# Winograd sums T3 and T2 and the first value weights prepared earlier in a hybrid attention block

## Chip, cores and metric

The kernel runs on one core of a Trainium2 chip. The metric is the device time of one execution in microseconds (us); the time of a version is the median of its runs.

## The reference, cut to what is computed

One decoder layer on 1024 tokens of width 1024. A normed input `h` is multiplied by one wide weight matrix; its columns feed a dilated attention (8 heads of 64), a gated linear recurrence (4 heads of 128) and two gates. The two branches are merged, then come a gated FFN, a gated embedding input and a last norm.

```python
h = rmsnorm(x, norm_mix[i])
proj = h @ w_in[i]
qa, ka, va, qb, fb, ib, gb, gate_a, gate_b = jnp.split(proj, IN_SPLITS, axis=-1)
ya = dilated_attention(qa, ka, va)
yb = hgrn2(qb, fb, ib, gb, lb_all[i], hg_norm[i])
merged = sigmoid(gate_a) * (ya @ w_a_up[i]) + sigmoid(gate_b) * (yb @ w_b_up[i])
x = x + merged @ w_out[i]
...
```

The part that matters here is `h @ w_in`. The kernel multiplies by the un-normed `x * norm_mix` and scales each token's result by its `rsqrt(mean(x*x) + EPS)`, called `rs`, afterwards.

## The kernel before

**Precision.** Every operand of a product is split in a high half (a cast on ScalarE, to fp32r) and a low half (source minus high half, on VectorE), and a product is three matmuls: high by high, high by low, low by high. The splits are the main work of ScalarE and VectorE, and the operand's matmuls wait for both.

**The start (lines 343 to 442).** Eight tiles `xr8[k]` of x (128 channels by 1024 tokens) are loaded and split with the gain; ScalarE squares them and VectorE adds the squares into `sqs`. Meanwhile TensorE computes three gate tiles, then a fourth (`w_next`, banks `pt1` and `pt0`). `rstd_rep` (line 207) makes `rs`: for each half of the tokens one matmul with ones (L209) into a bank of PSUM, two ScalarE reads of that bank (L210, an Abs_reciprocal_sqrt, whose table is loaded first, and L211), and three VectorE steps of a Newton iteration (L203 to L205). Both halves use the same bank, `pt0`, so the second L209 must wait until both reads of the first are done. VectorE then empties the gate banks with `rs` (L439).

**The projection units (lines 279 to 340, 750 to 794).** Twenty tiles of the projections are computed in ten units of two tiles by Winograd's scheme: seven products of four blocks each, in the order 1, 5, 7, 2, 3, 4, 6. A unit is 7 products x 4 blocks x 3 matmuls = 84 matmuls of 512 columns. The right operands are made once, before and during the first unit, and kept for all ten: products 1, 2 and 3 use the split tiles as they are; 5 uses T1, 7 uses T3, 4 uses T4 and 6 uses T2, sums of quarters of the gained `xr8`:

```python
T1 = f[i][:, c1] - f[i][:, c0]            # VectorE, L245, into f[i][:, c0]
T3 = f[i + 4][:, c1] - f[i][:, c1]        # GpSimd, L249, into f[i][:, c1]
T2 = f[i + 4][:, c1] - T1                 # GpSimd, L261, into f[i + 4][:, c1]
T4 = f[i + 4][:, c0] - T2                 # VectorE, L262, into f[i + 4][:, c0]
```

Each is then split by `block` (line 232: cast L235 on ScalarE, low half L236 on VectorE). `start_rights(j, i)` (line 373) scales the tiles that it needs by `norm_mix` in place (L376) and makes block i of product j. The calls for product 5 stand ahead of `rs`'s use, those for 7, then 4 and 6, at line 753, behind the first unit's left operands. The left operands are sums of weights (GpSimd, L292 to L295), split as L299 and L300. The sum s34 (L293, L295) lies in the buffer that `sqs` held.

**After the units (lines 840 to 874).** `v_gemm(0, ...)` computes the values of the first four heads: eight tiles of 128 tokens, 24 matmuls of 256 columns each, 192 in all (L484 to L486), from two weight strips that `weight` loads, splits on GpSimd (L171) and on VectorE (L172). Then the first four attention rows (scores L525 and L526 into the one score bank `sp`, row maximum L538 on VectorE, exponential L542 on ScalarE, scaling L544 on GpSimd, transposes L565 on TensorE) run beside the next gate product.

**What sets the order.** The program is written once in Python; a scheduler in the framework orders the instructions of each engine by readiness in its own estimate, and every engine then runs its own list strictly in order. `issue_after` adds an order edge without a wait. A buffer is named by its slot number in a ring (`ring([41])` is slot 41), and a writer waits for the last reader of what lay in the slot before. The weight strips of the values lie before in the general rings: high halves in slots 3 and 4, which the last unit's left operands for products 7 and 2 use, and low halves in slots 8 and 6. Slot 8 also holds the result `e0` of the last unit until its store to DRAM is done.

Of the kernel before, what the change touches and what calls it, by code (L numbers as in the profile page):

```python
# [12 lines left out]
F32 = mybir.dt.float32  # L13
F32R = mybir.dt.float32r
U8 = mybir.dt.uint8
AF = mybir.ActivationFunctionType
# [4 lines left out]
P = 128  # L21
S = 1024
D = 1024
KD = D // P
# [20 lines left out]
SCALE_A, SCALE_B = 0.9, (1.6, 1.3, 1.3, 1.3, 1.0)  # L45
# [4 lines left out]
V_MIX, V_FFN, V_PLE, V_FIN, V_LB0, V_LB1, V_HGN = 0, 8, 16, 24, 32, 36, 40  # L50
# [65 lines left out]
def drain(gen):  # L116
    for _ in gen:
        pass
# [11 lines left out]
def block_kernel(ctx: ExitStack, tc: tile.TileContext, a: dict, out: bass.AP):  # L130
    nc = tc.nc
    pe, dve, act, pool = nc.tensor, nc.vector, nc.scalar, nc.gpsimd
# [7 lines left out]
    def ring(ids):  # L140
        return Ring(sb, [f"s{i}" for i in ids])
# [9 lines left out]
    ones = cp.tile([P, P], F32, name="ones")  # L151
    lmask = cp.tile([P, len(LEVELS), P // 2], U8, name="lmask")
    vec = cp.tile([P, NVEC], F32, name="vec")
# [12 lines left out]
    def weight(src, shape, hi_ring=None, lo_ring=None):  # L166
        raw = RAW.next(shape, F32, "wr")
        nc.sync.dma_start(raw, src)
        hi = (hi_ring or HI).next(shape, F32R, "wh")
        lo = (lo_ring or LO).next(shape, F32R, "wl")  # L170
        pool.tensor_scalar(hi, raw, 1.0, 0.0, ALU.mult, ALU.add)  # L171
        dve.tensor_sub(lo, raw, f32(hi))  # L172
        return hi, lo
# [33 lines left out]
    def rstd_rep(dst, sq, bank, inv, t1, t2, first=True):  # L207

        pe.matmul(bank, ones, sq, start=first, stop=True)  # L209
        act.activation(dst, bank, AF.Abs_reciprocal_sqrt, bias=eps, scale=inv)  # L210
        read = act.activation(t1, bank, AF.Identity, bias=eps, scale=inv)  # L211
        return read, newton(dst, t1, t2)
# [55 lines left out]
    RIGHT = {1: right_b11, 5: right_t1, 7: right_t3, 2: right_b21, 3: right_b22, 4: right_t4, 6: right_t2}  # L268
# [76 lines left out]
    MS = pring("pt0")  # L345
    TMP = ring([37, 38])
# [8 lines left out]
    xg, xr8 = [], []  # L355
    sqs = SQ.next([P, S], F32, "sqs")
    nc.scalar.dma_start(vec, a["vec"])
    scratch = cp.tile([P, 1], F32, name="scratch")
    act_engine = act.activation(scratch, eps, AF.Square).ins.engine

    warm = MS.next([P, 512], F32, "warm")
    for _ in range(WARM):
        pe.matmul(warm[:, :P], ones, ones, start=True, stop=True)
    w_start = [weight_parts(a["w_in"][20 + t], [P, KD, P]) for t in range(NTOGETHER)]
    both = ps.tile([P, 2, 512], F32, tag="sp", name="start")
    banks = [ps.tile([P, 512], F32, tag=t, name=f"start_{t}") for t in ("b0", "b1", "b2", "ov")]
# [5 lines left out]

    def start_rights(j, i):

        for k in {5: (i,), 7: (i + 4,)}.get(j, ()):
            act.activation(xr8[k], xr8[k], AF.Identity, scale=vec[:, V_MIX + k : V_MIX + k + 1])  # L376
        right[j][i] = RIGHT[j](xr8, i, 4, ring([TB[j][i]]))

    def latest(engine):

        return next(i for i in reversed(nc.cur_bb.bb.instructions) if i.engine == engine)
# [34 lines left out]
            nc.sync.dma_start(lm, a["lmask"])  # L416
            dve.tensor_copy(lmask, lm)

    rs = ring([46]).next([P, S], F32, "rs")
    t1, t2 = TMP.next([P, S], F32, "t"), TMP.next([P, S], F32, "t")  # L420
    for c in range(2):
        cs = slice(c * 512, c * 512 + 512)
        scale_read, _ = rstd_rep(rs[:, cs], sqs[:, cs], MS.next([P, 512], F32, "ms"), 1.0 / D, t1[:, cs], t2[:, cs])

    with tc.issue_after(last_sum.ins):
        w_next = weight(a["w_in"][20 + NTOGETHER], [P, KD, P], ring([45]), ring([48]))
        last_split = latest(last_sum.ins.engine)

    with tc.issue_after(last_split), tc.issue_after(last_square.ins):
        for i in range(4):  # L430
            start_rights(5, i)
    banks.append([ps.tile([P, 512], F32, tag=t, name=f"start_{t}") for t in ("pt1", "pt0")])
    for b, cs in zip(banks[-1], halves):
        gemm(b, w_next, xg, cs.start, 512, range(KD))
# [51 lines left out]
            pe.matmul(b, xl[:, ts_], hi[:, k % 4, :], start=False, stop=(k == KD - 1))  # L486
            yield 3 * 0.107

    def v_gemm(half, vs):
        wts = [weight(a["w_v"][half, j], [P, 4, 256]) for j in range(2)]  # L490
        for t in range(NTOK):
            if t % 2 == 0:
                vs.append(VR.next([P, 2, 4, 2, 64], F32R, "v"))
            v = vs[-1]
            b = MM.next([P, 512], F32, "mm")[:, :256]
            yield from nat_gemm(b, wts, t)
            bv = b.rearrange("p (h d) -> p h d", h=4)
            r = rn[:, t : t + 1]
            act.activation(v[:, t % 2, :, 0, :], bv, AF.Identity, scale=r)
            dve.scalar_tensor_tensor(  # L500
                v[:, t % 2, :, 1, :], bv, r, f32(v)[:, t % 2, :, 0, :], op0=ALU.mult, op1=ALU.subtract
            )
# [248 lines left out]
    with tc.issue_after(first_emptied.ins), tc.issue_after(scale_read.ins):  # L751
        proj_lead()
    with tc.issue_after(latest(last_sum.ins.engine)), tc.issue_after(scale_read.ins):
        for i in range(4):
            start_rights(7, i)
        for i in (3, 0, 1, 2):
            for j in (4, 6):
                start_rights(j, i)

    TG, EO = ring([37, 38, 39]), ring([40, 47, 8])  # L760

# [4 lines left out]

    rn = cp.tile([P, NTOK], F32, name="rn")
    for tiles in units:
        done = dict(proj_unit(right, TG))
        e0, e1 = (EO.next([P, S], F32, "pj") for _ in range(2))  # L770
        dve.tensor_add(e0[:, c1], done[3], done[6])
        dve.tensor_add(e1[:, c0], done[4], done[6])
        pool.tensor_add(e1[:, c1], done[7], done[6])
        if tiles[0] < 8:

            dve.scalar_tensor_tensor(e0[:, c0], done[2], -0.125, rs[:, c0], op0=ALU.mult, op1=ALU.mult)
            dve.scalar_tensor_tensor(e0[:, c1], e0[:, c1], -0.125, rs[:, c1], op0=ALU.mult, op1=ALU.mult)
        else:
            dve.tensor_mul(e0[:, c0], done[2], rs[:, c0])
            dve.tensor_mul(e0[:, c1], e0[:, c1], rs[:, c1])  # L780
        pool.tensor_mul(e1, e1, rs)
        if 8 <= tiles[0] < 16:
            hd = tiles[0] // 2 - 4
            k = EO.next([P, S], F32, "k")
            act.activation(e0, e0, AF.Sigmoid)
            pool.tensor_scalar(e0, e0, oml[:, hd : hd + 1], lb[:, hd : hd + 1], ALU.mult, ALU.add)
            pool.tensor_scalar(k, e0, -1.0, 1.0, ALU.mult, ALU.add)
            nc.sync.dma_start(hg_dram["k"][hd], k)
            for cs in halves:
                sg = EV.next([P, 512], F32, "sg")  # L790
                act.activation(sg, e1[:, cs], AF.Sigmoid)
                dve.tensor_mul(e1[:, cs], e1[:, cs], sg)
        for j, e in zip(tiles, (e0, e1)):
            nc.sync.dma_start(proj_dst(j), e)
        if tiles[0] == 6:

            diag = EO.next([P, NTOK, P], F32, "diag")
            rs3 = rs.rearrange("p (n t) -> p n t", n=NTOK)
            dve.tensor_mul(diag, rs3, ident.unsqueeze(1).to_broadcast([P, NTOK, P]))
            dve.tensor_reduce(out=rn, in_=diag, axis=mybir.AxisListType.X, op=ALU.add)  # L800
# [42 lines left out]
    MM = pring("b0", "b1", "b2")  # L843
    NB = ring([47]).next([P, S], F32, "nb")
    nc.sync.dma_start(NB, a["nb"])
    drain(v_gemm(0, vs[0]))
    RAW, HI, LO = ring([0, 1]), ring([3, 4]), ring([8, 6])
    rows = []
    add_gates(2)
    v_last = fill.add(v_gemm(1, vs[1]))  # L850
    fill.along(attend_rows(0, qk[0, 0], rows), SCALE_A)
    groups = [(p, h, g) for p in range(NPAIR) for h in range(2) for g in range(2)]
    for (p, h, g), after in zip(groups, groups[1:] + [None]):
        if (p, h, g) == (2, 0, 0):
# [537 lines left out]
```

## Time and profile before

| what | value |
|---|---|
| median of 3 runs (lowest, highest) | 1650.5 us (1648.26, 1650.99) |
| the profiled execution: time, span in the profile | 1653.13 us, 1651.3 us |
| TensorE (PE) busy | 1599.5 us, 97% of the span |
| VectorE (DVE), ScalarE (ACT), GpSimd (POOL) busy | 68%, 39%, 29% |
| mean granted clock of TensorE | 0.987 |

The profiled execution's own time is 1.8 us above its span. PE is the row to read: the others have room over the whole span, and what counts is where PE stands still and who ends that wait.

### The profile page before, as it was taken

The page shows a single profiled execution, that of the slowest core. Times are in us where ns is not written, and L with a number is a line of the kernel's source. Part 1 is how long each engine was busy: PE and PEld are TensorE (multiplying, and loading weights), DVE is VectorE, ACT ScalarE, POOL GpSimd, SP SyncE. Part 2 cuts the span into 40 slices and gives each one's busy share as a digit, 9 for nine tenths or more (in the row PEclk, how much of TensorE's full clock was granted, in tenths as well). Part 3 has the DMA queues.
Part 4 walks back from the last instruction along what each step waited for, and adds up shares of the span by engine and source line. Part 5 has one row for each costly group of instructions (what it writes and reads, how often), then busy time and mean ns, then how long its engine had stood idle before and what let it go on. Part 6 is the DMA issues. An engine that isn't in the chain of part 4 may idle for free.

```text
span 1651.3 us, 21727 instructions
## 1 busy us (share of the span) xinstructions
PE 1599.5 (97%) x7968; PEld 1334.9 (81%) x7968; DVE 1119.2 (68%) x1725; ACT 651.9 (39%) x1130; POOL 475.7 (29%) x357
## 2 busy tenths in 40 slices
PE   8899998999999999999998999999999999999996
PEld 7687776898897888888786878888888788878886
DVE  8855655568665567774648786667777757789536
ACT  6422333357653011532336333333333454454433
POOL 2555662223322111015353222223333201002214
PEclk9999998999999999999999999999999999999998
DMA  5233344223224232543434773224444677765102
GB/s 199 77 103 113 128 147 140 80 87 81 65 71 156 91 108 98 177 145 118 134 127 144 269 260 130 90 101 142 153 160 159 214 262 249 237 200 159 43 1 102
DMA packets 93419, 227.97 MB, mean 138 GB/s; under 512 B 10368, under 2 KB 19840, under 8 KB 93312
## 3 DMA queue, kind: packets, MB, share of 16 engines
q1 hardware_dynamic: 93168, 226.57, 41.3%
q8 instruction: 62, 1.02, 0.3%
q14 instruction: 45, 0.37, 0.1%
q10 hardware_dynamic: 144, 0.02, 0.0%
HBM read 164.16 MB, written 62.39 MB: 137 GB/s over the span
## 4 chain that ended last, share of the span: by engine, by line
PE 47%; DVE 6%; DMA 5%; issue 2%; POOL 1%; ACT 1%; SPq 0%; DVEq 0%; POOLq 0%
PE u L275 7%; PE u L276 7%; PE u L277 7%; PE mm L192 5%; PE mm L194 5%; PE mm L193 5%; PE dnb L275 2%; PE dnb L277 2%; PE dnb L276 2%; DVE B L236 1%; DMA s_dram<-ls 1%; PE g L666 1%; DMA ls<-w_dn 1%; DMA w<-s_dram 1%; DMA w<-w_dn 1%
## 5 line engine op out<-in xcount | busy, mean ns | idle before, releaser
L275 PE MATMUL u<-B,q 128*128 128x512 f32 x776 | 303.9, 394 | 8.3 <-ACT m L333 5.1
L276 PE MATMUL u<-B,q 128*128 128x512 f32 x776 | 304.3, 392 | 3.9 <-DVE B L236 3.9
L277 PE MATMUL u<-B,q 128*128 128x512 f32 x776 | 303.6, 391 | 2.9 <-DVE q L300 2.9
L275 PEld LDWEIGHTS u<-B,q 128*128 128x128 f32 x776 | 146.8, 189 | 44.1 <-ACT m L333 9.5
L276 PEld LDWEIGHTS u<-B,q 128*128 128x128 f32 x776 | 146.6, 189 | 35.3 <-DVE B L236 5.4
L277 PEld LDWEIGHTS u<-B,q 128*128 128x128 f32 x776 | 146.7, 189 | 34.1 <-DVE q L300 3.3
L192 PE MATMUL mm<-xh,wh 128*128 128x512 f32 (+1 forms) x352 | 138.6, 394 | 0.0
L299 ACT CAST q<-s 128x512 fp32r<-128x512 f32 x128 | 79.4, 622 | 148.9 <-PE u L277 132.9
L300 DVE TENSOR_TENSOR q<-s,q 128x512 fp32r<-128x512 f32 x128 | 107.3, 841 | 40.9 <-ACT q L299 40.1
L194 PE MATMUL mm<-xh,wl 128*128 128x512 f32 (+1 forms) x352 | 132.3, 376 | 0.1
L193 PE MATMUL mm<-xl,wh 128*128 128x512 f32 (+1 forms) x352 | 131.8, 374 | 0.0
L171 POOL TENSOR_SCALAR wh<-wr 128x1024 fp32r<-128x1024 f32 (+1 forms) x55 | 59.9, 1091 | 247.6 <-PE mm L193 104.7
L300 DVE TENSOR_TENSOR q<-w,q 128x512 fp32r<-128x512 f32 x96 | 91.9, 958 | 51.1 <-ACT q L299 51.0
L192 PE MATMUL mm<-h,wh 128*128 128x512 f32 (+1 forms) x296 | 114.7, 387 | 1.2 <-POOL wh L171 1.1
L193 PE MATMUL mm<-l,wh 128*128 128x512 f32 (+1 forms) x296 | 114.4, 386 | 0.9 <-DVE l L910 0.9
L194 PE MATMUL mm<-h,wl 128*128 128x512 f32 (+1 forms) x296 | 113.7, 385 | 0.0
L299 ACT CAST q<-w 128x512 fp32r<-128x512 f32 x96 | 59.7, 622 | 122.0 <-PE u L277 69.7
L544 POOL TENSOR_SCALAR p<-p,rd 128x128 f32<-128x128 f32 (+3 forms) x64 | 53.3, 835 | 143.3 <-DVE rd L543 123.8
L1103 POOL TENSOR_TENSOR us<-v 128x512 f32<-128x512 f32 x22 | 38.4, 1746 | 171.6 <-DVE v L337 158.7
L194 PEld LDWEIGHTS mm<-xh,wl 128*128 128x128 f32 x352 | 66.8, 190 | 12.0 <-DVE wl L172 0.5
L484 PE MATMUL mm<-wh,xh 128*128 128x256 f32 x256 | 76.4, 300 | 0.0
L294 POOL TENSOR_TENSOR s<-s,w 128x512 f32<-128x512 f32 x32 | 45.1, 1410 | 107.4 <-DVE s L292 88.2
(305 smaller groups left out, 3791.5 us busy)
## 6 DMA issues: line engine op xcount, KB each, us to landing
w<-w_gu SPq DMA_DIRECT2D x44, 512.0 KB, 3.9
t_dram<-t SPq DMA_DIRECT2D x44, 256.0 KB, 2.3
w<-w_in SPq DMA_DIRECT2D x20, 512.0 KB, 3.8
w<-w_dn SPq DMA_DIRECT2D x40, 256.0 KB, 3.3
st<-t_dram SPq DMA_DIRECT2D x20, 512.0 KB, 4.5
ls<-w_dn SPq DMA_DIRECT2D x32, 256.0 KB, 4.1
wr<-w_in SPq DMA_DIRECT2D x13, 512.0 KB, 3.7
sg_dram<-gt SPq DMA_DIRECT2D x24, 256.0 KB, 2.0
```

The source lines that it names most:

```text
L171: pool.tensor_scalar(hi, raw, 1.0, 0.0, ALU.mult, ALU.add)
L192: pe.matmul(dst, hi[:, k, :], xh[:, c0 : c0 + n], start=first and k == ks[0], stop=False)
L193: pe.matmul(dst, hi[:, k, :], xl[:, c0 : c0 + n], start=False, stop=False)
L194: pe.matmul(dst, lo[:, k, :], xh[:, c0 : c0 + n], start=False, stop=last and k == ks[-1])
L275: pe.matmul(dst, q[:, 0, k], bh, start=first and not more and k == 0, stop=False, skip_group_check=more)
L276: pe.matmul(dst, q[:, 0, k], bl, start=False, stop=False, skip_group_check=more)
L277: pe.matmul(dst, q[:, 1, k], bh, start=False, stop=end, skip_group_check=more)
L294: pool.tensor_sub(s2, s1, a11)
L299: act.copy(q[:, 0], left[m])
L300: dve.tensor_sub(q[:, 1], left[m], f32(q)[:, 0])
L484: pe.matmul(b, xh[:, ts_], hi[:, k % 4, :], start=(k == 0), stop=False)
L544: pool.tensor_scalar(pr[:, :n], pr[:, :n], rd, 0.0, ALU.mult, ALU.add)
```

## The change

It has two places.

At the start, all eight tiles are scaled in one go behind the last square, and the blocks for product 7 (T3) are made right behind those for product 5 (T1), ahead of the reads of the sums of squares. The sums T2, which T4 is made from, are made there too, on GpSimd, and handed on to `start_rights`. The blocks for 4 and 6 stay behind the first unit's left operands, in another order.

At the end of the units, the two weight strips of `v_gemm(0)` are loaded and split in the last unit, with slots of their own: 41 and 42 for the high halves, 43 and 44 for the low ones. These four held the T3 blocks, whose last reader is product 7 of the last unit. The first attention rows are ordered behind the last matmul of `v_gemm(0)`.

```diff
--- before.py
+++ after.py
@@ -360,7 +360,7 @@
 
     warm = MS.next([P, 512], F32, "warm")
     for _ in range(WARM):
-        pe.matmul(warm[:, :P], ones, ones, start=True, stop=True)
+        warm_up = pe.matmul(warm[:, :P], ones, ones, start=True, stop=True)
     w_start = [weight_parts(a["w_in"][20 + t], [P, KD, P]) for t in range(NTOGETHER)]
     both = ps.tile([P, 2, 512], F32, tag="sp", name="start")
     banks = [ps.tile([P, 512], F32, tag=t, name=f"start_{t}") for t in ("b0", "b1", "b2", "ov")]
@@ -372,9 +372,10 @@
 
     def start_rights(j, i):
 
-        for k in {5: (i,), 7: (i + 4,)}.get(j, ()):
-            act.activation(xr8[k], xr8[k], AF.Identity, scale=vec[:, V_MIX + k : V_MIX + k + 1])
-        right[j][i] = RIGHT[j](xr8, i, 4, ring([TB[j][i]]))
+        t2 = (xr8[i + 4][:, c1],) if j in (4, 6) else ()
+        right[j][i] = RIGHT[j](xr8, i, 4, ring([TB[j][i]]), *t2)
+
+    pe_engine = warm_up.ins.engine
 
     def latest(engine):
 
@@ -416,19 +417,31 @@
             nc.sync.dma_start(lm, a["lmask"])
             dve.tensor_copy(lmask, lm)
 
-    rs = ring([46]).next([P, S], F32, "rs")
-    t1, t2 = TMP.next([P, S], F32, "t"), TMP.next([P, S], F32, "t")
-    for c in range(2):
-        cs = slice(c * 512, c * 512 + 512)
-        scale_read, _ = rstd_rep(rs[:, cs], sqs[:, cs], MS.next([P, 512], F32, "ms"), 1.0 / D, t1[:, cs], t2[:, cs])
 
     with tc.issue_after(last_sum.ins):
         w_next = weight(a["w_in"][20 + NTOGETHER], [P, KD, P], ring([45]), ring([48]))
         last_split = latest(last_sum.ins.engine)
 
+
     with tc.issue_after(last_split), tc.issue_after(last_square.ins):
+        for k in range(KD):
+            act.activation(xr8[k], xr8[k], AF.Identity, scale=vec[:, V_MIX + k : V_MIX + k + 1])
+        scaled = latest(act_engine)
+    with tc.issue_after(scaled):
+        for j in (5, 7):
+            for i in range(4):
+                start_rights(j, i)
+            right_read, right_made = latest(act_engine), latest(last_sum.ins.engine)
         for i in range(4):
-            start_rights(5, i)
+            t2 = xr8[i + 4][:, c1]
+            pool.tensor_sub(t2, t2, xr8[i][:, c0])
+    rs = ring([46]).next([P, S], F32, "rs")
+    t1, t2 = TMP.next([P, S], F32, "t"), TMP.next([P, S], F32, "t")
+    with tc.issue_after(right_read), tc.issue_after(right_made):
+        for c in range(2):
+            cs = slice(c * 512, c * 512 + 512)
+            bank = MS.next([P, 512], F32, "ms")
+            scale_read, _ = rstd_rep(rs[:, cs], sqs[:, cs], bank, 1.0 / D, t1[:, cs], t2[:, cs])
     banks.append([ps.tile([P, 512], F32, tag=t, name=f"start_{t}") for t in ("pt1", "pt0")])
     for b, cs in zip(banks[-1], halves):
         gemm(b, w_next, xg, cs.start, 512, range(KD))
@@ -486,8 +499,8 @@
             pe.matmul(b, xl[:, ts_], hi[:, k % 4, :], start=False, stop=(k == KD - 1))
             yield 3 * 0.107
 
-    def v_gemm(half, vs):
-        wts = [weight(a["w_v"][half, j], [P, 4, 256]) for j in range(2)]
+    def v_gemm(half, vs, wts=None):
+        wts = wts or [weight(a["w_v"][half, j], [P, 4, 256]) for j in range(2)]
         for t in range(NTOK):
             if t % 2 == 0:
                 vs.append(VR.next([P, 2, 4, 2, 64], F32R, "v"))
@@ -751,11 +764,8 @@
     with tc.issue_after(first_emptied.ins), tc.issue_after(scale_read.ins):
         proj_lead()
     with tc.issue_after(latest(last_sum.ins.engine)), tc.issue_after(scale_read.ins):
-        for i in range(4):
-            start_rights(7, i)
-        for i in (3, 0, 1, 2):
-            for j in (4, 6):
-                start_rights(j, i)
+        for j, i in ((4, 3), (6, 3), (4, 0), (4, 1), (4, 2), (6, 0), (6, 1), (6, 2)):
+            start_rights(j, i)
 
     TG, EO = ring([37, 38, 39]), ring([40, 47, 8])
 
@@ -766,6 +776,9 @@
 
     rn = cp.tile([P, NTOK], F32, name="rn")
     for tiles in units:
+        if tiles == units[-1]:
+
+            w_v0 = [weight(a["w_v"][0, j], [P, 4, 256], ring([41 + j]), ring([43 + j])) for j in range(2)]
         done = dict(proj_unit(right, TG))
         e0, e1 = (EO.next([P, S], F32, "pj") for _ in range(2))
         dve.tensor_add(e0[:, c1], done[3], done[6])
@@ -843,12 +856,14 @@
     MM = pring("b0", "b1", "b2")
     NB = ring([47]).next([P, S], F32, "nb")
     nc.sync.dma_start(NB, a["nb"])
-    drain(v_gemm(0, vs[0]))
+    drain(v_gemm(0, vs[0], w_v0))
+    values_made = latest(pe_engine)
     RAW, HI, LO = ring([0, 1]), ring([3, 4]), ring([8, 6])
     rows = []
     add_gates(2)
     v_last = fill.add(v_gemm(1, vs[1]))
-    fill.along(attend_rows(0, qk[0, 0], rows), SCALE_A)
+    with tc.issue_after(values_made):
+        fill.along(attend_rows(0, qk[0, 0], rows), SCALE_A)
     groups = [(p, h, g) for p in range(NPAIR) for h in range(2) for g in range(2)]
     for (p, h, g), after in zip(groups, groups[1:] + [None]):
         if (p, h, g) == (2, 0, 0):
```

How the lists of the engines change, at three places (numbers in the names tell buffers apart).

ScalarE before the first unit, before the change: `B` are the blocks of T1, `rs` and `t` the two reads of each half of the sums of squares (`ms`), `q` the first left operand.

```order
L235 CAST B_54_384<-xr_19_177 128x512
L235 CAST B_55_389<-xr_23_207 128x512
L210 ACT_TABLE_LOAD
L210 ACTIVATE rs_44_349<-ms_47_352,eps_73 128x512
L211 ACTIVATE t_45_350<-ms_47_352,eps_73 128x512
L210 ACTIVATE rs_44_349<-ms_48_359,eps_73 128x512
L211 ACTIVATE t_45_350<-ms_48_359,eps_73 128x512
L299 CAST q_64_488<-w0_60_478 128x512
```

The same place now; B_51 to B_54 are the blocks of T3.

```order
L235 CAST B_50_376<-xr_23_207 128x512
L235 CAST B_51_380<-xr_12_110 128x512
L235 CAST B_52_384<-xr_15_147 128x512
L235 CAST B_53_388<-xr_19_177 128x512
L235 CAST B_54_392<-xr_23_207 128x512
L210 ACT_TABLE_LOAD
L210 ACTIVATE rs_55_399<-ms_58_402,eps_73 128x512
L211 ACTIVATE t_56_400<-ms_58_402,eps_73 128x512
L210 ACTIVATE rs_55_399<-ms_59_409,eps_73 128x512
L211 ACTIVATE t_56_400<-ms_59_409,eps_73 128x512
```

Four casts that read GpSimd's sums now stand between T1's casts and the reads of the sums of squares.

GpSimd before the first unit, before the change: the second sum of weights (`s34`), then T3 (L249) and T2 (L261) by turns, four of each.

```order
L293 TENSOR_TENSOR s34_63_483<-w0_60_478,w1_61_479 128x512
L295 TENSOR_TENSOR s34_63_483<-w0_60_478,s12_62_482 128x512
L249 TENSOR_TENSOR xr_12_110<-xr_27_237,xr_12_110 128x512
L261 TENSOR_TENSOR xr_27_237<-xr_27_237,xr_12_110 128x512
L249 TENSOR_TENSOR xr_15_147<-xr_31_264,xr_15_147 128x512
```

The end of the same piece now; T2's line is L437.

```order
L249 TENSOR_TENSOR xr_19_177<-xr_35_291,xr_19_177 128x512
L437 TENSOR_TENSOR xr_35_291<-xr_35_291,xr_19_177 128x512
L249 TENSOR_TENSOR xr_23_207<-xr_40_322,xr_23_207 128x512
L437 TENSOR_TENSOR xr_40_322<-xr_40_322,xr_23_207 128x512
L293 TENSOR_TENSOR s34_67_507<-w0_64_502,w1_65_503 128x512
L295 TENSOR_TENSOR s34_67_507<-w0_64_502,s12_66_506 128x512
```

The eight sums still alternate, and all stand ahead of s34 now.

TensorE behind the last unit, before the change: behind three first matmuls of the values (`mm`) stand the scores (`sp`) of the first four attention rows, a transpose (`pt`), and the first matmul that reads a low half of the value weights (`wl`).

```order
L525 MATMUL sp_2230<-kh_1924,q_1923 128x384
L526 MATMUL sp_2230<-kl_1925,q_1923 128x384
L525 MATMUL sp_2244<-kh_1924,q_1923 128x512
L526 MATMUL sp_2244<-kl_1925,q_1923 128x512
L565 MATMUL pt_2277<-ident,p_2198 128x128
L485 MATMUL mm_1976<-wl_1966,xh_111 128x256
L486 MATMUL mm_1976<-wh_1965,xl_112 128x256
```

Now, from the last matmul of the last unit on:

```order
L277 MATMUL u_1824<-B_531,q_1860 128x512
L497 MATMUL mm_1976<-wh_1813,xh_111 128x256
L498 MATMUL mm_1976<-wl_1814,xh_111 128x256
L499 MATMUL mm_1976<-wh_1813,xl_112 128x256
L497 MATMUL mm_1976<-wh_1813,xh_148 128x256
L498 MATMUL mm_1976<-wl_1814,xh_148 128x256
```

The 192 matmuls of the values now run in one piece, and the scores stand behind them. On VectorE the two low halves of the value weights (`wl_1814`, `wl_1820`) moved from among the first rows' maxima to ahead of the last unit's sum of products 7 and 5:

```order
L487 TENSOR_TENSOR q_1954<-qr_1959,q_1954 64x512
L172 TENSOR_TENSOR wl_1814<-wr_1811,wh_1813 128x1024
L172 TENSOR_TENSOR wl_1820<-wr_1817,wh_1819 128x1024
L335 TENSOR_TENSOR v_1827<-u_1825,m_1826 128x512
L792 TENSOR_TENSOR pj_1925<-u_1823,rs_399 128x512
```

On the DMA queue of SP the loads of the value weights keep their places; the loads of the next two gate weights come six issues earlier, and on GpSimd their splits stand ahead of the last unit's two sums instead of behind the first rows.

## Rows read from the trace of the kernel before

**Rows 1.** PE's waits, 0 to 330 us: line, releaser: us in total, times, longest us
```profile
PE u L276 <- DVE B L236: 3.3, 2, 3.0
...
PE sp L525 <- DVE m L538: 1.6, 3, 0.7
```

**Rows 2.** PE in order of time, first projection unit: start us, us, line, instruction [idle <-releaser]
```profile
56.29 0.39 PE L275 MATMUL u<-xh,q 128*128 128x512 f32 x1
...
65.35 0.59 PE L276 MATMUL u<-B,q 128*128 128x512 f32 x1 [3.04 <-DVE B L236]
...
69.89 0.39 PE L275 MATMUL u<-xh,q 128*128 128x512 f32 x1
...
75.36 0.39 PE L275 MATMUL u<-B,q 128*128 128x512 f32 x1
...
78.87 0.50 PE L277 MATMUL u<-B,q 128*128 128x512 f32 x1 [2.89 <-DVE q L300]
...
85.65 0.39 PE L275 MATMUL u<-xh,q 128*128 128x512 f32 x1
```

**Rows 3.** Stretches: us, busy us (count) of each engine, PEclk, DMA share, GB/s
```profile
65.35:68.90 3.55, 3.31 (x7) 2.12 (x8) 3.55 (x5) 2.24 (x6) 1.67 (x2) 0.54 0.03 10
85.65:264.45 178.80, 174.25 (x758) 142.48 (x756) 107.16 (x129) 57.42 (x95) 101.45 (x60) 0.99 0.37 128
136.18:139.03 2.85, 2.85 (x13) 2.36 (x13) 2.85 (x4) 0.00 (x0) 0.47 (x1) 1.00 0.00 0
212.09:215.44 3.35, 3.35 (x9) 2.60 (x9) 2.06 (x3) 0.47 (x1) 2.13 (x2) 0.55 0.89 341
280.83:301.10 20.27, 20.27 (x171) 20.27 (x170) 4.18 (x9) 3.86 (x8) 1.05 (x1) 1.00 0.01 3
```

**Rows 4.** PE in order of time: two stalls of later units
```profile
136.18 0.50 PE L275 MATMUL u<-xh,q 128*128 128x512 f32 x1 [1.27 <-DVE v L335]
...
212.09 0.56 PE L275 MATMUL u<-B,q 128*128 128x512 f32 x1 [2.31 <-ACT m L333]
```

**Rows 5.** ScalarE in order of time, 26 to 50 us
```profile
27.78 4.25 ACT L376 ACTIVATE xr<-xr,vec 128x1024 f32<-128x1024 f32 x4
...
39.32 0.62 ACT L235 CAST B<-xr 128x512 fp32r<-128x512 f32 x1 [1.84 <-DVE xr L245]
39.96 1.28 ACT L210 ACT_TABLE_LOAD   x1
44.71 0.69 ACT L210 ACTIVATE rs<-ms,eps 128x512 f32<-128x512 f32 x1 [3.47 <-PE ms L209]
```

**Rows 6.** VectorE in order of time, 33 to 70 us
```profile
34.94 1.88 DVE L245 TENSOR_TENSOR xr<-xr 128x512 f32<-128x512 f32 x3
...
63.55 4.63 DVE L236 TENSOR_TENSOR B<-xr,B 128x512 fp32r<-128x512 f32 x4
```

**Rows 7.** GpSimd in order of time: first T3 sum and last T2 sum
```profile
53.52 1.30 POOL L249 TENSOR_TENSOR xr<-xr,xr 128x512 f32<-128x512 f32 x1 [1.94 <-ACT xr L376]
...
64.83 1.60 POOL L261 TENSOR_TENSOR xr<-xr,xr 128x512 f32<-128x512 f32 x1
```

**Rows 8.** PE in order of time: second matmul of the sums of squares
```profile
47.48 1.02 PE L209 MATMUL ms<-sqs,ones 128*128 128x512 f32 x2
```

**Rows 9.** ScalarE in order of time: a table load and what follows it
```profile
167.55 1.28 ACT L785 ACT_TABLE_LOAD   x1
168.84 1.06 ACT L785 ACTIVATE pj<-pj 128x1024 f32<-128x1024 f32 x1
```

**Rows 10.** PE in order of time: from last unit to the end of the values
```profile
264.45 0.51 PE L484 MATMUL mm<-wh,xh 128*128 128x256 f32 x3
...
276.52 0.58 PE L485 MATMUL mm<-wl,xh 128*128 128x256 f32 x1 [0.59 <-DVE wl L172]
...
301.10 0.41 PE L192 MATMUL mm<-xh,wh 128*128 128x512 f32 x1
```

**Rows 11.** VectorE in order of time: second low half of value weights
```profile
275.15 1.31 DVE L172 TENSOR_TENSOR wl<-wr,wh 128x1024 fp32r<-128x1024 f32 x1
```

## Prediction

> **What bounds the kernel now.** The page gives the bound: PE is busy nearly all of the span, so only what PE stands still for can be won. I read PE's waits first, over the stretch that the change touches, 0 to 330 us [rows 1]: the reader is to see that the long ones have VectorE as their releaser, the low halves of blocks `B` (L236) and the row maxima (L538). Then PE in order of time, at the two places.
>
> *Place 1, the first projection unit* [rows 2]. It begins at 56.29 and the next at 85.65: 29.36 us. In it, 24 matmuls from 69.89 to 75.36 without a wait give 0.228 us each, so 84 would take 19.15 us. The unit loses 10.2 us: a stop of 3.04 us at product 7 (a block of T3 is late), one of 2.89 us at product 4 (a left operand's low half, which stands in VectorE's list behind the blocks of T4 and T2), and a slow stretch behind each. Those stretches are at a granted clock of 0.54, about 1.2 GHz, right behind the stop [rows 3]: 3.55 us x (1 - 0.54) = 1.6 us lost. The nine units behind run with PE busy 174.25 of 178.80 us [rows 3], so time won in the first is not taken back there by another engine.
>
> *Place 2, behind the last unit* [rows 10]. From 264.45, the values' first matmuls, to 301.10, the first gate matmul behind them, 36.65 us pass. At full clock 171 matmuls of 256 columns took 20.27 us [rows 3], 0.1185 each. The 192 of the values are 22.75 us; the four rows' scores, 2 x (256 + 256 + 384 + 512) = 2816 columns, are 1.3 us at that rate; a transpose is some 0.1. So 12.5 us are lost. The values' matmul at 276.52 waits for the low half that VectorE made at 275.15 to 276.46 [rows 11]: its slot 8 held a result whose store had to land first.
>
> **Place 1 now, step by step.** Scaling eight tiles: four take 4.25 us from 27.78 [rows 5], about 1.05 a step, so eight end at 36.2. Before, ScalarE waited for T1 from 32.03, so the four more fill idle time and push T1's casts from 35.65 to 36.2: nothing, since product 5 is needed 20 us later.
>
> T3 and T2 on GpSimd: the first T3 needs T1's first subtraction done, a third of the 1.88 us from 34.94 [rows 6], so 35.6. The eight took from 53.52 to 66.43, starts 1.62 apart with VectorE working beside them, 1.30 for the first alone [rows 7]. The last T3 is the seventh: it ends at 35.6 + 7 x 1.6 = 46.8; at 1.36 each it would be 45.2, at 1.75 each 47.9.
>
> That is a new wait. ScalarE's list holds T3's last cast, then the table load, then the reads of the sums of squares: 46.85 + 0.62 + 1.28 [rows 5] puts the first read at 48.75, where it was 44.71, and two reads end near 50.0. The second matmul of the sums of squares, now at 47.48 [rows 8], shares the bank and waits for them. PE's list is in order, so the fourth gate tile behind it waits too: **PE stops for about 2.5 us**, 0.9 and 3.6 by the two other speeds of GpSimd. GpSimd's s34 waits for that matmul as it does now and so stays ahead of its use by the same margin; VectorE's Newton steps, the emptying of the banks and the first low halves hang on the same reads and shift with PE.
>
> The clock behind that stop: after 1.27 us it stayed at 1.00, after 2.31 us it fell to 0.55 [rows 3, 4]. I take a fall, 1.6 us as above; the other end is 0.
>
> On the table load a page speaks against the change. The row shows 1.28 us, and elsewhere the next activation starts 0.01 us behind such a load [rows 9]. The Trainium skill, ScalarE: Activation LUTs, "What ACT_TABLE_LOAD costs", adds a drain of some 1.38 us to each, 2.66 in all; by that the stop would be 3.9 us. Today's load here ends long before its reader may start, so only the other row bears on it; I go by the rows.
>
> What becomes free: T3's four low halves, 4.63 us at 63.55 [rows 6], leave VectorE's list between the left operands and T4, and GpSimd no longer works beside what is left there. From the start of product 1 to product 4 five products pass, 60 x 0.228 = 13.7 us. In them VectorE has five left low halves, two bank readings, four T4 and six low halves to do, 17 of a kind that takes 0.6 alone (1.88 for three, rows 6): 10.2 us. It fits, so the stop at product 4 goes as well as that at product 7.
>
> Place 1: 10.2 - 2.5 - 1.6 = **6.1 us won**; 9.3 with the short stop at full clock, 4.9 with the long one and 1.7 for the clock.
>
> **Place 2 now.** The strips' loads are not moved. Slots 41 to 44 are free after product 7 of the last unit, half a unit before its end, so the two splits on GpSimd and the two on VectorE (1.31 us in rows 11) are done some 5 us before the values begin. Passed on VectorE: the last unit's sums, whose readers are stores that nothing near waits for, and whose banks the values don't use. Passed on SP and GpSimd: the gate weights now stand ahead of key loads and of the last sums. The latest of the chain behind them is a half of a key tile, loaded behind the last unit's stores, and it must be split before the values' fourth tile is emptied; the values' 22.75 us cover it. Nothing else of that reordering has a price.
>
> The scores now stand behind the values. Their waits for row maxima stay, up to the 1.6 us of today [rows 1]; a table load falls among them, and gate matmuls now stand between them as cover. I take 0.9, with 0 and 1.6 as ends. The stretch becomes 22.75 + 1.3 + 0.1 + 0.9 = 25.05 us, **11.6 us won** (12.5 and 10.9).
>
> **Sum.** 6.1 + 11.6 = 17.7 us. The profiled execution, 1651.3 of span and 1653.13 in all, would be 1635.4; the median shown is 2.6 below it, and the same gain from 1650.5 gives **1632.8 us**. The ends are 1650.5 - 21.8 = 1628.7 and 1650.5 - 15.8 = 1634.7.
>
> **The rivals.**
>
> *VectorE still paces product 4.* For: under GpSimd its 512-column operations took 4.63 / 4 = 1.16 us [rows 6]; 17 of them are 19.7 us against 13.7 of cover, PE stops 6 us and loses 1.6 more to the clock. Against: GpSimd has only two sums of the next unit's weights to do there. All of it gives 1632.8 + 7.6 = 1640.4. Chance 0.12.
>
> *The drain.* The load holds ScalarE 1.38 us longer, so the second sum matmul, PE and all behind it come that much later: 1634.2. That is the page's rule above. The pair at 167.55 and 168.84 [rows 9] speaks against it. Chance 0.05.
>
> *The values' weights come no earlier.* The high halves' slots are waited for until the last product, or the second strip's load is late; then place 2 stays and only place 1 counts: 1650.5 - 6.1 = 1644.4. Against: their last reader is product 7, and the load's place in the queue is the old one. Chance 0.06.
>
> *Slower: a store in VectorE's way.* The low half of the next gate weight still goes to slot 8, behind the store of the last unit's result, and now stands in VectorE's list ahead of the values' third emptying. PE has three banks for the values and needs that one back at its sixth tile, 5 x 2.85 = 14.2 us after 264.45. If the store lands later than that, PE stops for the difference; 18 us of it would eat both gains, and 25 us give 1650.5 - 17.7 + 25 = 1657.8. Today that low half is made at 275.15 [rows 11], some 3 us before the point. Chance 0.02.
>
> **How the numbers follow.** The forecast has what is left, 0.75. Its own ends, 1628.7 and 1634.7, are widened by the spread of the runs shown and by the first rival at the upper end: 1627 to 1641, which leaves out the third and fourth rival and tails. A measurement of this kernel can tell about 0.2%, 3.3 us. Faster 0.95; the same 0.03 (place 2 failing with a long stop at place 1); slower 0.02.
>
> **What would show it.** PE: a stop of 1 to 3.6 us at the second L209, with ScalarE's second read as its releaser; no stop for `B` or `q` in the first unit; 192 matmuls of the values in one piece of 22.8 us directly behind the last unit. ScalarE: T3's last cast near 47, the table load right behind it. A first unit of over 22 us, or a stop among the values, would make the forecast wrong.

## The result and the profile after

The changed kernel takes **1633.1 us** (median of 4 runs, 1630.84 to 1634.88) against 1650.7 for the kernel before in the same session; the ratio is 0.9895, 95% interval 0.9882 to 0.9907. The forecast was 1632.8, in a range of 1627 to 1641. The profiled execution took 1633.63 us with a span of 1631.9, 19.4 under the span before.

PE's waits of the changed kernel, 0 to 330 us (line, releaser: us in total, times, longest us):

```profile
PE u L275 <- ACT m L333: 3.3, 2, 2.3
PE ms L209 <- ACT t L211: 3.2, 1, 3.2
PE u L275 <- DVE v L335: 1.9, 2, 1.3
```

The waits for blocks `B`, for a left operand `q`, for row maxima and for a low half of the value weights [rows 1, 2, 10] are gone. So are the two longest waits behind the last unit of the kernel before, where the first attention row's scores stood ahead of the values and PE waited for the two halves of the keys:

```profile
267.40 0.58 PE L525 MATMUL sp<-kh,q 128*128 128x256 f32 x1 [2.45 <-ACT kh L472]
270.07 0.58 PE L526 MATMUL sp<-kl,q 128*128 128x256 f32 x1 [2.08 <-DVE kl L475]
```

All of PE's waits from there until the values go on at 276.52 come to 6.9 us, 4.5 of them for keys, and the granted clock was 0.58 from 264.45 to 280.71. One wait is new, at the second matmul of the sums of squares. PE of the changed kernel in order of time (start, us, line, instruction, idle before and its releaser):

```profile
43.34 1.02 PE L209 MATMUL ms<-sqs,ones 128*128 128x512 f32 x2
...
50.50 1.45 PE L209 MATMUL ms<-sqs,ones 128*128 128x512 f32 x2 [3.18 <-ACT t L211]
...
61.07 0.39 PE L275 MATMUL u<-xh,q 128*128 128x512 f32 x1
...
80.11 0.39 PE L275 MATMUL u<-xh,q 128*128 128x512 f32 x1
...
258.29 0.28 PE L497 MATMUL mm<-wh,xh 128*128 128x256 f32 x1
...
281.33 0.28 PE L538 MATMUL sp<-kh,q 128*128 128x256 f32 x1
...
288.07 0.48 PE L192 MATMUL mm<-xh,wh 128*128 128x512 f32 x1
```

The first unit runs from 61.07 to 80.11, 19.04 us where it took 29.36 [rows 2]; the second unit starts 5.5 us earlier. The values run from 258.29 to 281.33 in one piece. The last line is the matmul of the next gate's seventh block; before, the same one stands here:

```profile
306.55 0.48 PE L192 MATMUL mm<-xh,wh 128*128 128x512 f32 x1
```

From the values' first matmul to it, 42.10 us (264.45 to 306.55) became 29.78: 12.3 us won. The two places give 5.5 and 12.3, and units 2 to 10 another 0.6 (178.80 to 178.18); some 0.9 us of the 19.4 between the spans lie behind 288 us and are not taken apart. The stretches as windows (us; busy us and count of PE, PEld, DVE, ACT, POOL; PEclk; DMA share; GB/s):

```profile
50.50:54.60 4.10, 4.10 (x9) 2.79 (x10) 3.85 (x6) 2.62 (x5) 2.57 (x2) 0.58 0.00 0
61.07:80.11 19.04, 19.04 (x86) 15.77 (x84) 16.97 (x26) 8.97 (x16) 9.43 (x4) 1.00 0.36 126
80.11:258.29 178.18, 172.97 (x757) 141.32 (x756) 109.71 (x132) 57.42 (x95) 104.21 (x62) 1.00 0.38 132
258.29:281.33 23.04, 23.04 (x194) 23.03 (x193) 11.91 (x19) 6.65 (x13) 4.03 (x2) 1.00 0.52 158
```

PE is busy for the whole of the first unit and of the values. Behind the new stop the clock is low, at 0.58 for 4.10 us. What stands before that stop, on GpSimd (first and last T3) and then on ScalarE (T3's last cast, the table load, the two reads):

```profile
35.43 1.61 POOL L249 TENSOR_TENSOR xr<-xr,xr 128x512 f32<-128x512 f32 x1 [2.96 <-DVE xr L245]
...
45.49 1.73 POOL L249 TENSOR_TENSOR xr<-xr,xr 128x512 f32<-128x512 f32 x1
```

```profile
47.25 0.62 ACT L235 CAST B<-xr 128x512 fp32r<-128x512 f32 x1 [2.77 <-POOL xr L249]
47.89 1.28 ACT L210 ACT_TABLE_LOAD   x1
49.18 0.69 ACT L210 ACTIVATE rs<-ms,eps 128x512 f32<-128x512 f32 x1
49.77 0.68 ACT L211 ACTIVATE t<-ms,eps 128x512 f32<-128x512 f32 x1
```

### The profile page after: what moved, and what is told of

It is laid out like the page before. It is cut to its first block, busy times and chain, and to the rows that moved or that the text cites. A ratio compares the mean times of both kernels' runs of the same rounds, so it can differ in the third digit from the quotient of the medians.

```text
span 1631.9 us, 21724 instructions
## 1 busy us (share of the span) xinstructions
PE 1592.2 (98%) x7968; PEld 1331.2 (82%) x7968; DVE 1119.7 (69%) x1725; ACT 651.5 (40%) x1130; POOL 475.9 (29%) x357
## 4 chain that ended last, share of the span: by engine, by line
PE 49%; DVE 6%; DMA 4%; issue 2%; POOL 1%; ACT 1%; SPq 0%; DVEq 0%; POOLq 0%; ACTq 0%
PE u L275 7%; PE u L277 7%; PE u L276 7%; PE mm L192 5%; PE mm L194 5%; PE mm L193 5%; PE dnb L275 2%; PE dnb L277 2%; PE dnb L276 2%; DVE B L236 1%; PE g L679 1%; DMA s_dram<-ls 1%; DMA ls<-w_dn 1%; DMA st<-first_dram 1%; POOL sb L941 1%
```

## The experiments

**One place alone.** Two kernels, each with one of the change's places. The first is the changed kernel with its second place taken back; the second has these same lines put into the kernel before, and nothing at the start.

```diff
-        if tiles == units[-1]:
-            w_v0 = [weight(a["w_v"][0, j], [P, 4, 256], ring([41 + j]), ring([43 + j])) for j in range(2)]
-    drain(v_gemm(0, vs[0], w_v0))
+    drain(v_gemm(0, vs[0]))
-    with tc.issue_after(values_made):
-        fill.along(attend_rows(0, qk[0, 0], rows), SCALE_A)
+    fill.along(attend_rows(0, qk[0, 0], rows), SCALE_A)
```

Start only. 

> Only the change at the start (scalings in one go, T3 and T2 ahead of the reads of the sums of squares); the value weights and the scores are as before. Theory A, the two places are independent: the first unit's gain of after stays (second unit 5.5 us earlier than before) and the stretch behind the last unit takes its old 36.65 us, so 1650.7 - 5.5 = 1645.2 us (1644.3 to 1646.0). Rival B, the first unit's gain is given back downstream without the other part: 1650 to 1651. Rival C, part of what was won behind the last unit comes from the start (freed engines): under 1643.

Behind the last unit only. 

> Only the change behind the last unit (value weights split in the last unit with slots 41 to 44, scores ordered behind the values), the start as before. Theory A, independent places: first unit 29.4 us as before, values in one piece of 23.0 us, time 1650.7 - 12.3 = 1638.4 us (1637.4 to 1639.2); 12.3 is what the stretch to the gate matmul with its seventh block gave in after. Rival B: the values' weights are late here because slots 41 to 44 or the engines come free later; a stop at the first value matmul and 1640 or more.

Measured on one chip, beside 1648.12 for the kernel before: start only 1644.12 us (ratio 0.9979, 0.9969 to 0.9988), the other 1636.59 (0.9932, 0.9915 to 0.9948). The kernel before was 2.6 us faster on this chip than in the session of the result, so the expected times don't compare, but the gains do: 4.0 and 11.5 us by the medians where 5.5 and 12.3 were expected. They come to 15.5; the change as a whole won 16.3 to 17.6 in three sessions (ratios 0.9895, 0.9903, 0.9900, each known to some 2 us). The places are independent as far as this can be measured, and the second carries about three quarters. Why the first gave less than 5.5 is taken up with the table further down. In the kernel with the start as it was, PE waits at the old places:

```profile
PE u L276 <- DVE B L236: 3.0, 1, 3.0
...
PE u L277 <- DVE q L300: 1.8, 1, 1.8
```

**The weights or the order of the scores?** The changed kernel with the value weights put back into the general slots, the scores still ordered behind the values:

```diff
-            w_v0 = [weight(a["w_v"][0, j], [P, 4, 256], ring([41 + j]), ring([43 + j])) for j in range(2)]
...
-    drain(v_gemm(0, vs[0], w_v0))
+    drain(v_gemm(0, vs[0]))
     values_made = latest(pe_engine)
```

> After, with the value weights loaded and split where they were (general slots), the scores still ordered behind the values. Theory A, the weights' slots and time are what counts: the second low half needs the buffer of the last unit's result, whose store lands some 4 us behind its making, so PE stops at the first matmul that reads it for 4 to 10 us; 1637 to 1643 us. Rival B, the gain behind the last unit is only that the values' matmuls no longer stand behind the scores, which wait for keys and row maxima: 1633 us, no stop over 1 us among the values.

It took 1643.34 us (0.9972, 0.9961 to 0.9984), hardly better than the start alone. PE's longest wait, then VectorE around it:

```profile
PE mm L498 <- DVE wl L172: 8.0, 1, 8.0
```

```profile
255.35 1.22 DVE L172 TENSOR_TENSOR wl<-wr,wh 128x1024 fp32r<-128x1024 f32 x1
...
260.68 4.50 DVE L488 TENSOR_TENSOR kl<-kl,kh 128x512 fp32r<-128x512 f32 x4
265.10 1.21 DVE L172 TENSOR_TENSOR wl<-wr,wh 128x1024 fp32r<-128x1024 f32 x1
```

The late low half is the first strip's, the one for slot 8. VectorE starts it at 265.10 without idle time before it: what held it then was its place in the list, behind four low halves of keys, not the store itself. The kernel before shows the same: its low half at 275.15 [rows 11] starts without idle time, behind two low halves of keys. To order the scores behind the values without earlier weights only exchanges one wait for another; in the lists of the changed kernel, on the other hand, taking that order out alters not one row on any engine, so it contributes nothing there.

The other half of the question: slots 41 to 44 kept, but the weights called for behind the last unit, where `v_gemm` stood.

```diff
-        if tiles == units[-1]:
-            w_v0 = [weight(a["w_v"][0, j], [P, 4, 256], ring([41 + j]), ring([43 + j])) for j in range(2)]
...
+    w_v0 = [weight(a["w_v"][0, j], [P, 4, 256], ring([41 + j]), ring([43 + j])) for j in range(2)]
     drain(v_gemm(0, vs[0], w_v0))
```

> After, with the two value weights' call written behind the last unit again, but kept in slots 41 to 44 (and the scores ordered behind the values). Theory A, what counts is the slots, since the framework's scheduler moves a free split forward by itself: values in one piece of 23.0 us without a wait, the time of after within 1.5 us. Rival B, the place in the program counts: the low halves come behind the last unit's sums on VectorE, PE stops at the first matmul that reads one, 3 us or more over after.

It took 1632.06 us (0.9909, 0.9896 to 0.9923) beside 1631.92 for the changed kernel on that chip, and its low halves are made at 247.69 and 250.17, in the last unit. The scheduler moves the splits forward by itself once their slots are free. Here too the lists are the same, row for row, without the order edge on the scores: **the four slots are the whole of the second place.** With the values' low halves early, the values stand ahead of the scores, and the keys have the values' 23 us to be ready.

**The stop at the start.** The changed kernel with T2 ordered behind all T3; `latest` gives GpSimd's last instruction so far, by a list `made` of its weight splits:

```diff
+        last_t3 = latest(made[-1].ins.engine)
+    with tc.issue_after(last_t3):
         for i in range(4):
             t2 = xr8[i + 4][:, c1]
             pool.tensor_sub(t2, t2, xr8[i][:, c0])
```

> After, with the four sums T2 on GpSimd ordered behind all four sums T3. Theory A, the stop at the second matmul of the sums of squares comes from T2 standing between the T3 sums on GpSimd: last T3 ends 3 x 1.7 = 5 us earlier, near 42.2, its cast by 43, the table load by 44.2, both reads by 45.8, before that matmul is reached (47.3). The stop of 3.18 us and the slow stretch behind it (4.10 us at a granted clock of 0.58, 1.7 us lost) go: 1633.1 - 4.9 = 1628.2 us (1627.5 to 1629). Rival B, the table load and T3's casts alone keep the reads late: the stop stays at 1.5 us or more, 1630 to 1632. Rival C, the stop goes but VectorE then paces a later product of the first unit (products 4 and 6), which gives 2 us or more back: 1630 to 1633.

It took 1634.52 us (0.9919, 0.9904 to 0.9934): no gain. The stop is gone as theory A said (ScalarE's table load at 42.51, the first read at 43.81), and another wait stands in its place, then a second. PE's waits, and VectorE:

```profile
PE u L275 <- DVE gt L454: 4.2, 1, 4.2
...
PE u L277 <- DVE q L300: 1.7, 1, 1.7
```

```profile
34.31 4.69 DVE L245 TENSOR_TENSOR xr<-xr 128x512 f32<-128x512 f32 x4
38.91 13.67 DVE L236 TENSOR_TENSOR B<-xr,B 128x512 fp32r<-128x512 f32 x8
52.51 0.68 DVE L203 TENSOR_TENSOR t<-rs 128x512 f32<-128x512 f32 x1
```

The reads of the first half are over at 45.1, but its Newton steps start only at 52.51: eight low halves of blocks take 13.67 us, 1.7 each, with GpSimd at work all that time. The unit then waits for the banks that `rs` empties (rival C, though before product 1 and not at 4 or 6). In the changed kernel these low halves end at 50.6, hardly behind the reads of the first half (50.45), so the stop hid them. Theory A's 1628.2 left out this second chain.

So the next edit takes GpSimd out of this stretch: T3 and T2 on VectorE.

```diff
-        for j in (5, 7):
-            for i in range(4):
-                start_rights(j, i)
-            right_read, right_made = latest(act_engine), latest(last_sum.ins.engine)
+        for i in range(4):
+            t1 = xr8[i][:, c0]
+            dve.tensor_sub(t1, xr8[i][:, c1], t1)
+        for i in range(4):
+            t3 = xr8[i][:, c1]
+            t3_made = dve.tensor_sub(t3, xr8[i + 4][:, c1], t3).ins
+    with tc.issue_after(t3_made):
+        for j, cs in ((5, c0), (7, c1)):
+            for i in range(4):
+                right[j][i] = block(ring([TB[j][i]]), xr8[i][:, cs])
+            right_read, right_made = latest(act_engine), latest(last_sum.ins.engine)
+    with tc.issue_after(right_made):
         for i in range(4):
             t2 = xr8[i + 4][:, c1]
-            pool.tensor_sub(t2, t2, xr8[i][:, c0])
+            dve.tensor_sub(t2, t2, xr8[i][:, c0])
```

> After, with the eight sums T3 and T2 made by VectorE instead of GpSimd, T1 and T3 first, then the eight low halves, then T2. Theory A, VectorE is slow between 35 and 52 us because GpSimd works beside it (1.7 us for a 512-column operation that takes 0.6 alone): 20 operations then take some 12 us instead of 8 and 4 in 18, T3's last cast ends near 40.5, the reads follow the first sums-of-squares matmul at once, no stop at the second one over 1 us, no wait for an emptied bank; the second unit starts some 32 us behind that first matmul, and the time is 4 to 8 us under after in this call. Rival B, operations on VectorE stay at 1.2 us or more there; 20 of them end near 58, PE stops 4 us or more for an emptied bank, slower than after.

It took 1627.61 us (0.9881, 0.986 to 0.9903), 4.3 under the changed kernel on that chip, with intervals that overlap. VectorE now does twelve sums and eight low halves, twenty operations, from 34.6 to 46.7, where the twelve that it has in the changed kernel end at 50.6:

```profile
34.62 2.48 DVE L433 TENSOR_TENSOR xr<-xr 128x512 f32<-128x512 f32 x4
37.03 2.48 DVE L436 TENSOR_TENSOR xr<-xr,xr 128x512 f32<-128x512 f32 x4
39.43 4.89 DVE L236 TENSOR_TENSOR B<-xr,B 128x512 fp32r<-128x512 f32 x8
44.25 2.48 DVE L445 TENSOR_TENSOR xr<-xr,xr 128x512 f32<-128x512 f32 x4
46.66 0.68 DVE L203 TENSOR_TENSOR t<-rs 128x512 f32<-128x512 f32 x1
```

Each takes 0.6, so rival B falls. The first unit starts at 55.97, the second at 75.40, 32 us behind the first matmul of the sums of squares, without a wait of PE between. In a second session with the changed kernel, each for a further set of runs:

> The version with the sums T3 and T2 on VectorE again, unchanged, as the candidate that beats both kernels. Theory A: its second unit follows the arrival at the first matmul of the sums of squares by some 32 us, so 72.5 to 75.5; 4 to 8 us under after in this call, ratio to before 0.985 to 0.988. Rival B: the lead of the first call (4.3 us between medians, with intervals that overlap) was chance; the two versions lie within 2 us.

> After a third time, beside the version with all eight sums on VectorE. By what the runs before this one show: ratio 0.9895 to 0.9905, second unit between 80.0 and 81.2 us whatever the arrival at the first matmul of the sums of squares.

1627.61 us (0.9866, 0.9851 to 0.9881) against 1632.88 (0.9900, 0.9883 to 0.9916): **5.3 us faster than the changed kernel**, the best version of this study, and its slowest run there (1628.5) is faster than the other's fastest (1630.7). But theory A's start of the second unit, 72.5 to 75.5, was missed: it came at 77.27, 36 us behind the arrival at 41.13. PE came to the first unit earlier there, at 54.02, and waited 2.2 us for the low half of the first left operand, with a granted clock of 0.68 behind that wait (56.92 to 60.00). VectorE made this low half at 56.19, where the profile of the first session has it at 55.90: its list did not move forward with the arrival, and two of its Newton steps took 1.59 and 1.67 us instead of 0.69, beside GpSimd's s34. So this version too has a chain with an end of its own.

T3 alone on VectorE, T2 left on GpSimd (`start_rights(7, i)` with `dve.tensor_sub`, the rest as in the changed kernel). 

> After, with T3 alone on VectorE and T2 left on GpSimd. By theory A of the run with all sums on VectorE the four T2 sums still slow VectorE from some 38 to 45 us: T3's last cast near 46, a stop of 0 to 4 us at the second matmul of the sums of squares; time between after and that run. By rival B slower than after.

1630.27 us (0.9895, 0.988 to 0.991), between the two by the medians, though its interval overlaps both, and not for the reason given: VectorE was not slowed. GpSimd's first T2, and VectorE beside it:

```profile
37.71 7.09 POOL L442 TENSOR_TENSOR xr<-xr,xr 128x512 f32<-128x512 f32 x1 [5.31 <-DVE xr L378]
```

```profile
38.76 4.29 DVE L236 TENSOR_TENSOR B<-xr,B 128x512 fp32r<-128x512 f32 x7
42.97 0.68 DVE L378 TENSOR_TENSOR xr<-xr,xr 128x512 f32<-128x512 f32 x1
44.34 1.01 DVE L236 TENSOR_TENSOR B<-xr,B 128x512 fp32r<-128x512 f32 x1 [0.69 <-ACT B L235]
```

Seven low halves at 0.6 each, while one sum on GpSimd takes 7.09 us, to 44.80, and ends only behind VectorE's first pause (43.65 to 44.34). T2 then lasts to 49.9 and pushes s34, and PE waits 1.7 us for a left operand.

**How much of the start's gain hangs on the run.** 

> After once more, unchanged, beside the runs that follow. The runs so far show that TensorE reaches the first matmul of the sums of squares at 40.6 to 43.7 us, a spread that the loads at the start give. Theory A, in after the second unit's start no longer follows that arrival but the chain ScalarE, VectorE, GpSimd up to T3's last cast (80.1 to 81.2 us whatever the arrival), while before it follows the arrival by 40.5 to 42 us: an arrival at 41 then costs a stop of some 5 us at the second such matmul, and the gain over before on such a run is 14 us where it was 17.5; ratio 0.990 to 0.9915. Rival B, the gain does not hang on the arrival: second unit 36.8 us behind the first such matmul as in the first profile, ratio 0.9895 again.

1631.92 us (0.9903, 0.9888 to 0.9919). Its profile came to the first matmul of the sums of squares late, at 43.26, so this run by itself tells nothing; the profiles of all runs that have the start of before or of the changed kernel tell more (us, read from PE in order of time; the stop is the one at the second such matmul):

```
kernel                     first L209   stop   second unit starts
before                       43.66      none      85.65
start as before              40.63      none      81.09
changed                      43.34      3.18      80.11
changed, second session      43.26      3.19      80.06
changed, third session       41.88      4.77      81.11
start only                   41.69      4.79      81.20
weights in general slots     41.40      4.81      80.56
slots kept, called late      40.51      5.36      80.67
```

With the start as before, the second unit follows PE's arrival by 40.5 to 42 us in the two profiles at hand. With the change it starts at 80.1 to 81.2 whatever the arrival: the chain over scalings, T1, T3, table load and reads ends at its own time (the second such matmul starts at 49.85 to 50.62 in all six), and the stop takes up the difference. An early arrival therefore wins nothing more, and beside a start such as that of the second row the first place wins about nothing; beside the profiled execution of before it won 5.5. The 4.0 us of the start alone, a median over many runs, lies between. What sets the arrival was not tested; the expectation puts it down to the loads. Run times alone could not separate this: their spread on one chip is 3 to 9 us.

## Why the prediction was right, step by step

**The cover at the first unit held.** With the waits for `B` and `q` gone it takes 19.04 us against the 19.15 worked out. VectorE does not pace product 4, the first rival: from 63.91 on its operations take 0.6 each, with GpSimd idle until 69.3.

**The new stop was seen and sized 0.7 us short**: 3.18 for 2.5. T3's last sum ended at 47.2 for 46.8, since a GpSimd sum took 1.68 us from start to start for the 1.6 taken; the first read came at 49.18 for 48.75. The clock's fall behind it cost 4.10 x (1 - 0.58) = 1.7 us for 1.6. Of 10.3 us recovered, 3.2 and 1.7 are given back: 5.4 left, 5.5 measured, 6.1 forecast.

**The step that was missing** is what fixes the end of that chain. The sum took the arrival at the second matmul from one execution and gave the stop one size. The stop is 3.2 to 5.4 us and the gain 5.5 to about none, by the arrival.

**How much was luck.** The median came out 0.3 us from the forecast, and errors that cancel have their part in it: by the profiles the first place was taken 0.6 too high and the second 0.7 too low. The profiled execution, forecast at 1635.4, took 1633.63, since 1.5 us more were won in the later units and behind 288 us, which the sum had at nothing. And both profiled executions, the one that the forecast was read from and the one that it is compared with here, came to the sums of squares late, at 43.66 and 43.34.

**The drain did not happen.** The table load ended at 49.17 and the first read began at 49.18. The Trainium skill, ScalarE: Activation LUTs, "What ACT_TABLE_LOAD costs", adds a drain of some 1.38 us to each load; here, where the load started 0.02 us behind the end of the cast ahead of it (47.87), and a reader stood directly behind and PE waited for that, there was 0.01 us. The trace does not agree with the Trainium skill on this.

**The second place was sized 0.7 us short**: 12.3 for 11.6. The values took 23.04 us for 22.75, and the row waits, taken at 0.9, are nil: gate matmuls stand between the scores. The rival of the store in VectorE's way did not come about: the next gate weight's low half was made at 265.15, between the values' second and third emptying, and VectorE was idle again before the third. The prediction named the low half (0.6 us) and the row maxima (1.6) as what PE waited for there and passed over the keys (4.5); the sum did not suffer, because it set the whole stretch against the work in it. And the forecast spoke of slots, an earlier place and the scores' order together; the slots alone do it, and of the store that it named for slot 8 the trace shows no wait, only a place in VectorE's list.

**Why VectorE and GpSimd hold each other up.** The prediction used 0.6 us alone and 1.16 under GpSimd as two prices without asking when each is paid. GpSimd adds two weights in the changed kernel's second session as s34 while VectorE goes through `rs`:

```profile
52.10 1.75 POOL L293 TENSOR_TENSOR s<-w,w 128x512 f32<-128x512 f32 x1 [3.28 <-PE ms L209]
53.82 1.74 POOL L295 TENSOR_TENSOR s<-w,s 128x512 f32<-128x512 f32 x1
```

```profile
52.81 0.69 DVE L452 TENSOR_TENSOR gt<-start,rs 128x512 f32<-128x512 f32 x1
...
54.51 1.60 DVE L204 SCALAR_TENSOR_TENSOR t<-t,t 128x512 f32<-128x512 f32 x1
```

The emptying of a bank, with one operand in PSUM, keeps its 0.69 us beside GpSimd; the Newton step, with both operands in SBUF, starts at 54.51 and ends at 56.11, 0.55 behind the end of GpSimd's sum (55.56). The Trainium skill, SBUF — State Buffer, "Who interferes with whom", states that a VectorE instruction with two SBUF inputs contends with a GpSimd instruction that reads SBUF, that the lock on the port which they share is exclusive, and that the order of issue decides who is blocked. The rows above agree on the exclusion: in the run with T3 first the two alternate, 1.7 us each. On the order they agree only in part: in the run with T3 alone on VectorE, GpSimd's sum stands in the trace from 37.71, nine VectorE operations that start after it run one behind the other, and GpSimd is the one held, for 7.09 us. Why the two alternate in one run and not in the other is open; no run was made for it.

## What to carry to other kernels

Work moved ahead of a wait must end before what the wait stood for, and its end must be followed over every engine that it crosses; a stop that takes up another chain's slack is worth nothing until that chain is shortened too. A sum of two SBUF tiles on GpSimd beside such sums on VectorE was no help here: 20 operations on VectorE alone took 12 us, and the same 20 with 8 of them on GpSimd took 16 to 18. Where a split is late, look first at who holds its slot: a free slot let the scheduler do the moving by itself.

## What the runs showed of the hardware that was not expected

Two engines that exclude each other did not always take turns: the same kind of sum took GpSimd 1.7 us where the two alternated and 7.09 us where VectorE ran without a pause. And the time at which PE reaches the sums of squares differs by over 3 us between executions (40.51 to 43.66), which is as much as one of the stops that were priced here.
